# Paged attention in a hybrid decoder step: the transposed, scaled probabilities made by transposes and an add, in place of a matmul with a scaled pattern

## The chip, the core and the metric

The kernel runs on one core of a Trainium2 chip, in one launch. The metric is the device time of a whole execution in microseconds (us), the median of several runs. A core has a matmul engine (TensorE, PE in the profile, with its weight loads as PEld), a vector engine (VectorE, DVE), a scalar engine (ScalarE, ACT), GpSimd (POOL), a sync engine that issues DMAs (SyncE, SP) and 16 DMA engines. Each engine takes its instructions in program order and waits on semaphores where another engine's result is needed. PE writes only to PSUM, eight banks of 512 fp32 columns on 128 partitions.

## The reference

Two layers of a decoder step over 256 prompt rows and 64 sample rows (8 sequences of 8 tokens), width 2048. A layer projects its input with one matrix, runs three mixers side by side, projects their outputs, and ends with a gated feed-forward block. The change is in the second mixer, for the sample rows:

```
# _diff_attn_sample, 4 heads, two maps of 64 dims per head, 1024 cached keys in 8 pages
s_past = einsum('bqhmd,bkhmd->bhmqk', q, k_past) * scale
s_new  = einsum('bqhmd,bkhmd->bhmqk', q, k) * scale
p  = softmax(concat([s_past, s_new]))            # with a causal mask on the new keys
pd = p[:, :, 0] - lam * p[:, :, 1]               # the two maps
o  = einsum('bhqk,bkhv->bqhv', pd[..., :P], v_past) + einsum(..., pd[..., P:], v)
```

The other two mixers are a gated delta rule (six heads) and a gated linear attention (six heads, "GLA"). The output projection starts with the outputs of the delta rule and of this attention, and needs those of GLA for its second half.

## The kernel before

**Dense work.** All weight matrices stream through SBUF in blocks of 128x512 fp32, 217 of them for a layer's input projection and 1618 in all; one of each layer's 217 is in a form of its own and not split. A block is split into a high and a low part, `whi` by a cast on ScalarE and `wlo` by a subtraction on VectorE (line 1021), and used by 12 matmuls of 320 columns, high by high, high by low and low by high. These are the *dense* matmuls here, PE rows with `whi` or `wlo`. Blocks are loaded some eight ahead of use and split three or four ahead.

**Mixers.** The mixers are generators that advance between the dense matmuls while the program is written. They never stand still for each other in the text; what orders them is data, SBUF space and PSUM banks. The cached-key attention (`attn_scores`, line 2049, and `attn_values`, line 2121) takes the eight sequences in four pairs. For a pair it computes scores on 128 partitions (head, sequence, map, query), exponentiates into `e` (128x1088: 1024 cached keys and 64 new ones), and then needs `PT`: keys on the partitions, 64 columns (sequence, head, query), scaled by the softmax sums and with the two maps subtracted. Before the change one matmul for each page does that at once: `e` is the stationary operand and the moving one is a 128x64 pattern of zeros and ones whose rows are scaled. `attn_values` multiplies `PT` with the cached values, two pairs at a time ("a quad"), page by page as the value pages land in a ring of three buffers.

**What follows the attention.** The delta rule of the sample rows, `gdn_sample` (line 1795), is run for two groups of three heads. In the second group the score products `sq,sk` of its third head are written to the PSUM bank that the attention's last transpose has left, and GLA (`gla_main`, line 2172) takes the SBUF space that the attention frees. After its scores and a small triangular inverse, `gdn_sample` takes its three heads in turn in one buffer of 128x1024: the head's state is loaded, multiplied (`gen,sq` and `gen,sk`), updated, stored, and the next one is loaded over it. GLA takes levels (1, 2, 4 and so on), each with subtractions, an exponential, multiplications, some 60 small products and predicated copies. A last step, `gate` (line 1533), multiplies the delta rule's output with its gate into `oA`.

**Order.** When all instructions are recorded, `Program.order` (line 536) sorts them with a list scheduler that uses the costs and latencies written in the file, and `issue` (line 691) emits them in that order on every engine. A dense matmul therefore has a fixed place among the mixers' matmuls, and PE does not go past one that waits. The first dense matmul of the output projection reads `oA`; it stands behind the 216 dense blocks of the input projection, that is behind 2592 dense matmuls.

```
            for f in ((("oA", l), ("oB", l)) if hf == 0 else (("oC", l),)):
                drain(f)
```

Of the kernel before, what the change touches and what calls it, by code (L numbers as in the profile page):

```python
# [18 lines left out]
ALU = mybir.AluOpType  # L19
# [49 lines left out]
def shape_consts(past_len):  # L69
    c = Cols()  # L70
    p = np.arange(128)
    j, i = p[:, None], p[None, :]
    c.add("ident", np.eye(128))
    c.add("tri", j <= i)
    c.add("tri16", (j <= i) / 16.0)
    j8, i8 = np.arange(64)[:, None], np.arange(128)[None, :] % 64
    same8 = (j8 // 8) == (i8 // 8)
    c.add("tri8d", same8 & (j8 <= i8))
    c.add("bo8d", same8)
    c.add("tri8_16", (same8 & (j8 <= i8))[:, :64] / 16.0)  # L80
    c.add("ind8", ((p[:, None] % 64) // 8) == np.arange(8)[None, :])
    c.add("mneg", np.where(i >= j, 0.0, NEG))
    c.add("mneg8", np.where((same8 & (i8 >= j8))[:, :64], 0.0, NEG))
    mcz = np.zeros((128, 256))
    mcz[:, 128:] = np.where(i <= j, 0.0, NEG)
    c.add("mcz", mcz)
    j32, i32 = p[:, None] % 32, np.arange(32)[None, :]
    ms = [(j32 // (2 * s) == i32 // (2 * s)) & (j32 % (2 * s) < s) & (i32 % (2 * s) >= s) for s in (1, 2, 4, 8, 16)]
    c.add("ms", np.stack(ms, 1))
    c.add("m4", ((p[:, None] % 32) // 8) == np.arange(4)[None, :])  # L90
    h, b2, m, q = p // 32, (p // 16) % 2, (p // 8) % 2, p % 8
    cc = np.arange(64)
    c.add("pat", (b2[:, None] == cc[None] // 32) & (h[:, None] == (cc[None] // 8) % 4) & (q[:, None] == cc[None] % 8))
    c.add("sel0", m[:, None] == 0)
    c.add("sel1", m[:, None] == 1)
    t = np.arange(64)
    mnew = [np.where((t[None] // 8 == 2 * pr + b2[:, None]) & (t[None] % 8 <= q[:, None]), 0.0, NEG) for pr in range(4)]
    c.add("mnew", np.stack(mnew, 1))
    c.add("idb", j32 == i32)
    inv = (1.0 / (np.float32(500000.0) ** (np.arange(8, dtype=np.float32) * np.float32(2.0) / np.float32(16.0)))).astype(np.float32)  # L100
    pos = np.concatenate([np.arange(NPR), np.tile(past_len + np.arange(8), 8)]).astype(np.float32)
    ang = (pos[:, None] * inv[None, :]).astype(np.float32)
    cos, sin = np.cos(ang).T, np.sin(ang).T
    C, S = np.ones((128, NT)), np.zeros((128, NT))
    for mm in range(2):
        C[64 * mm:64 * mm + 8] = cos
        C[64 * mm + 8:64 * mm + 16] = cos
        S[64 * mm:64 * mm + 8] = -sin
        S[64 * mm + 8:64 * mm + 16] = sin
    c.add("cos", C)  # L110
    c.add("sin", S)
    c.add("e6", np.full((128, 1), 1e-6))
    c.add("e5", np.full((128, 1), 1e-5))
    c.add("one", np.ones((128, 1)))
    c.add("mhalf", np.full((128, 1), -0.5))
    c.add("i2048", np.full((128, 1), 1.0 / 2048))
    c.add("i512", np.full((128, 1), 1.0 / 512))
    ci = Cols()
    ci.add("mi", np.stack([j32 == i32] + ms, 1))
    return c, ci  # L120
# [623 lines left out]
def emit(nc, pool, psp, T, O, coff, ioff, n_pages):  # L744
# [7 lines left out]
    NPG = n_pages // 8  # L752
# [22 lines left out]
    banks = [psp.tile([128, 512], F32, name=f"bank{i}") for i in range(8)]  # L775
# [32 lines left out]
    def cs(name, rows=slice(0, 128)):  # L808
        a, n = coff[name]
        return cst[rows, a:a + n]  # L810


    def mm(out, lhsT, rhs, start=True, stop=True):
        PE.matmul(out, lhsT, rhs, start=start, stop=stop, skip_group_check=True)

    def tr(out, in_, rows=slice(0, 128)):
        k = rows.stop - rows.start
        a, _ = coff["ident"]
        PE.transpose(out, in_, cst[rows, a + rows.start:a + rows.start + k])

    def tt(eng, out, a, b, op):
        eng.tensor_tensor(out=out, in0=a, in1=b, op=op)
# [4 lines left out]
    def tsc(eng, out, a, s1_, op0, s2_=None, op1=None):  # L827
        if s2_ is None:
            eng.tensor_scalar(out=out, in0=a, scalar1=s1_, scalar2=None, op0=op0)
        else:  # L830
            eng.tensor_scalar(out=out, in0=a, scalar1=s1_, scalar2=s2_, op0=op0, op1=op1)
# [73 lines left out]
    def bank(n=1):  # L905
        if clk.task.t > clk.t["PE"] + SLACK:
            yield
        while len(dense_free if wide[0] else mix_free) < n:
            yield WAIT
        bs = [(dense_free if wide[0] else mix_free).popleft() for _ in range(n)]  # L910
        for b_ in bs:
            prog.epoch(f"bank{b_}")
        return bs if n > 1 else bs[0]

    def fb(*bs):
        for b in bs:
            free_dense(b)
# [1131 lines left out]
    def attn_scores(l, lsel, getb, get1):  # L2049
        X = L  # L2050
        q, ring = X["kv"]
        EH = yield from get1(1024 + 64 + 64)
        e = ap(EH)
        QDs = []
        for i in range(2):
            QD = yield from getb(256)
            G.memset(ap(QD), 0.0)
            QDs.append(QD)
        X["PT"] = {}
        X["PTfree"] = deque()  # L2060
        for i in range(2):
            X["PTfree"].append((yield from getb(576)))
        for pr in range(4):

            qd = ap(QDs[pr % 2]).rearrange("p (h e c) -> p h e c", h=4, e=2)
            for e2 in range(2):
                for m in range(2):
                    r = slice(64 * m, 64 * m + 64)
                    c = e2 * 16 + m * 8
                    t0 = 256 + (2 * pr + e2) * 8  # L2070
                    (G if m else V).tensor_copy(qd[r, :, e2, c:c + 8], blkB[r, 0:4, t0:t0 + 8])
            yield
            bs = yield from bank(2)
            for pg in range(0, NPG, 2):
                for b2 in range(2):
                    KT = yield from kv_next(q[0])
                    kt = ap(KT).rearrange("p (a h t) -> p h a t", a=2, h=4)
                    c0 = (pg % 4) * 128
                    for h in range(4):
                        mm(banks[bs[pg // 4]][32 * h:32 * h + 32, c0:c0 + 256], qd[:, h, b2, :], kt[:, h], b2 == 0, b2 == 1)  # L2080
                    ring.append(KT)
                yield
            bn = yield from bank()
            for b2 in range(2):
                for h in range(4):
                    mm(banks[bn][32 * h:32 * h + 32, 0:64], qd[:, h, b2, :], blkB[:, 4 + h, 256:320], b2 == 0, b2 == 1)
            sm = yield from getb(8)
            s = ap(sm)
            for i in range(2):
                V.tensor_reduce(out=s[:, i:i + 1], in_=banks[bs[i]], op=ALU.max, axis=AX.X)  # L2090
            tt(V, e[:, 1024:1088], banks[bn][:, 0:64], cs("mnew")[:, pr * 64:pr * 64 + 64], ALU.add)
            fb(bn)
            V.tensor_reduce(out=s[:, 2:3], in_=e[:, 1024:1088], op=ALU.max, axis=AX.X)
            V.tensor_reduce(out=s[:, 3:4], in_=s[:, 0:3], op=ALU.max, axis=AX.X)
            tsc(V, s[:, 3:4], s[:, 3:4], -0.125, ALU.mult)
            for i in range(2):
                A.activation(e[:, 512 * i:512 * i + 512], banks[bs[i]], AF.Exp, scale=0.125, bias=s[:, 3:4], accum_out=s[:, i:i + 1])
            A.activation(e[:, 1024:1088], e[:, 1024:1088], AF.Exp, scale=0.125, bias=s[:, 3:4], accum_out=s[:, 2:3])
            fb(*bs)
            V.tensor_reduce(out=s[:, 4:5], in_=s[:, 0:3], op=ALU.add, axis=AX.X)  # L2100
            V.reciprocal(s[:, 5:6], s[:, 4:5])
            tt(V, s[:, 5:6], s[:, 5:6], lsel, ALU.mult)
            tsc(V, e[:, 1088:1152], cs("pat"), s[:, 5:6], ALU.mult)
            fr(sm)
            yield
            while not X["PTfree"]:
                yield WAIT
            PT = X["PTfree"].popleft()
            pt_ = ap(PT)
            bb = yield from bank(2)  # L2110
            for pg in range(NPG):
                mm(banks[bb[0]][:, pg * 64:pg * 64 + 64], e[:, pg * 128:pg * 128 + 128], e[:, 1088:1152])
            mm(banks[bb[1]][0:64, 0:64], e[:, 1024:1088], e[:, 1088:1152])
            A.copy(pt_[:, 0:512], banks[bb[0]])
            V.tensor_copy(pt_[0:64, 512:576], banks[bb[1]][0:64, 0:64])
            fb(*bb)
            X["PT"][pr] = (PT, clk.task.t)
            yield
        set_flag(("asc", l))
# [514 lines left out]
```

## Time and profile before

| | |
|---|---|
| median of 3 runs | 3294.72 us (3292.67 to 3296.1) |
| the profiled execution, its own time | 3294.52 us |
| its span, first to last instruction | 3292.7 us |
| PE busy | 3235.2 us (98%) |
| VectorE, ScalarE, GpSimd busy | 1959.6, 1493.2, 359.7 us |
| mean granted clock of TensorE | 0.994 |

The span is what the trace covers; 1.8 us of the execution's time lie around it. A busy PE is the union of its instructions' times, and their ends overlap, so the distance between two starts tells more of PE's pace than the time of one.

### The profile page before, as it was taken

Reading aid. Unit: us, or ns where it says so; the run is one execution under the profiler, and the core shown is the slowest. Engines: PE = TensorE matmul, PEld = TensorE weight load, DVE = VectorE, ACT = ScalarE, POOL = GpSimd, SP = SyncE. Lnnn points to the kernel's source line nnn. Section 1 sums busy time; section 2 is a strip of 40 time slices with the busy share of each in tenths; the row PEclk is TensorE's granted clock in tenths of the full one; section 3 lists DMA queues with packets and bytes.
Section 4 is the critical chain, followed back from the end, with each engine's and each line's share of the span. In section 5 each row is a group of like instructions: output and inputs, shape, how many; then the busy total and the mean of one; then the engine's idle time right before and its main releaser. Section 6 shows DMA issues by size and latency. Waiting matters only on the chain.

```text
span 3292.7 us, 67703 instructions
## 1 busy us (share of the span) xinstructions
PE 3235.2 (98%) x25466; PEld 3072.3 (93%) x25466; DVE 1959.6 (60%) x3780; ACT 1493.2 (45%) x3069; POOL 359.7 (11%) x604
## 2 busy tenths in 40 slices
PE   9999999999999999999999999989999999999997
PEld 9987887899999999999999887878999999999997
DVE  5676558885444445544776764588854544454446
ACT  5454444465433443344574444444744334433444
POOL 0233323200000000000002333231000000000000
PEclk9999999999999999999999999999999999999998
DMA  7466764455555555555555667534555555555553
GB/s 228 142 194 212 220 194 129 137 148 157 151 149 150 151 151 148 151 150 151 150 154 154 193 217 231 170 127 138 147 151 151 151 149 150 151 150 149 150 151 115
DMA packets 264393, 527.70 MB, mean 160 GB/s; under 512 B 31362, under 2 KB 33026, under 8 KB 263938
## 3 DMA queue, kind: packets, MB, share of 16 engines
q1 hardware_dynamic: 243586, 456.26, 48.4%
q0 software_dynamic: 20480, 67.13, 6.3%
q8 instruction: 199, 3.26, 0.4%
q14 instruction: 128, 1.05, 0.1%
HBM read 506.25 MB, written 16.36 MB: 159 GB/s over the span
## 4 chain that ended last, share of the span: by engine, by line
PE 76%; issue 2%; DVE 1%; DMA 1%; ACT 0%; POOL 0%; POOLq 0%; SPq 0%; ACTq 0%; DVEq 0%
PE bank L696 76%; DVE gen L696 0%; POOLq L2029 0%; DMA geng<-in_ck 0%; DVE wlo L696 0%; DVE geng L696 0%; POOL geng L2031 0%; DVE blkB L696 0%; DMA out_gs<-gen 0%; DMA gen<-in_sgdn 0%; DMA c<-in_sgdn 0%; ACT blkB L696 0%; DVE c L696 0%; POOL blkB L696 0%; ACT accq L696 0%
## 5 line engine op out<-in xcount | busy, mean ns | idle before, releaser
L696 DVE TENSOR_TENSOR wlo<-raw,whi 128x512 fp32r<-128x512 f32 x1616 | 1124.2, 696 | 1091.4 <-PE bank L696 893.5
L696 ACT CAST whi<-raw 128x512 fp32r<-128x512 f32 x1616 | 1001.7, 620 | 1403.6 <-PE bank L696 1340.0
L696 PE MATMUL bank<-xh,wlo 128*128 128x320 f32 (+1 forms) x4544 | 1418.6, 312 | 0.0
L696 PE MATMUL bank<-xh,whi 128*128 128x320 f32 (+1 forms) x4544 | 1413.3, 311 | 4.7 <-ACT xh L696 4.7
L696 PE MATMUL bank<-xl,whi 128*128 128x320 f32 (+1 forms) x4544 | 1414.6, 311 | 0.1
L696 PEld LDWEIGHTS bank<-xh,whi 128*128 128x128 f32 x4544 | 856.1, 188 | 12.8 <-issue 5.7
L696 PEld LDWEIGHTS bank<-xh,wlo 128*128 128x128 f32 x4544 | 857.8, 189 | 7.6 <-issue 3.9
L696 PEld LDWEIGHTS bank<-xl,whi 128*128 128x128 f32 x4544 | 855.4, 188 | 7.6 <-issue 4.4
L696 PE MATMUL bank<-actA,whi 128*128 128x320 f32 x1152 | 255.5, 309 | 0.0
L696 PEld LDWEIGHTS bank<-actA,whi 128*128 128x128 f32 x1152 | 192.9, 188 | 0.4
L696 PE MATMUL bank<-actA,wlo 128*128 128x320 f32 x576 | 178.1, 309 | 0.0
L696 PE MATMUL bank<-actB,whi 128*128 128x320 f32 x768 | 170.5, 309 | 0.0
L696 PE MATMUL bank<-actCh,whi 128*128 128x320 f32 x448 | 138.3, 309 | 0.0
L696 PE MATMUL bank<-actCl,whi 128*128 128x320 f32 x448 | 138.3, 309 | 0.0
L696 PE MATMUL bank<-actCh,wlo 128*128 128x320 f32 x448 | 138.3, 309 | 0.0
L696 PEld LDWEIGHTS bank<-actB,whi 128*128 128x128 f32 x768 | 128.6, 188 | 0.0
L696 PE MATMUL bank<-actB,wlo 128*128 128x320 f32 x384 | 118.6, 309 | 0.0
L696 PE MATMUL bank<-geng,gen 128*32 128x256 f32 (+5 forms) x968 | 101.8, 466 | 7.3 <-DMA geng<-in_ck 4.4
L696 PEld LDWEIGHTS bank<-actA,wlo 128*128 128x128 f32 x576 | 108.2, 188 | 0.1
L696 POOL COPY gen<-g 128x24 f32<-128x24 f32 x18 | 5.9, 328 | 878.1 <-DMA g<-in_scv 871.2
L2031 POOL DMA_DIRECT2D geng<-in_ck x128 | 70.7, 552 | 274.3 <-DVE actA L696 137.8
L696 PE MATMUL bank<-oA,whi 128*128 128x320 f32 x384 | 92.7, 325 | 5.3 <-ACT oA L696 4.8
(291 smaller groups left out, 3324.1 us busy)
## 6 DMA issues: line engine op xcount, KB each, us to landing
raw<-in_wgu SPq DMA_DIRECT2D x704, 256.0 KB
raw<-in_win SPq DMA_DIRECT2D x434, 256.0 KB
raw<-in_wd SPq DMA_DIRECT2D x352, 256.0 KB
geng<-in_ck POOLq DMA_DIRECT2D x128, 256.0 KB, 3.8
geng<-in_cvp POOLq DMA_DIRECT2D x128, 256.0 KB, 3.7
raw<-in_wout SPq DMA_DIRECT2D x128, 256.0 KB
c<-in_sgdn SPq DMA_DIRECT2D x6, 512.0 KB
out_gs<-c SPq DMA_DIRECT2D x6, 512.0 KB
```

Source lines behind the costliest of these rows:

```text
L696: fn(*[real(x) for x in a], **{k: real(v) for k, v in kw.items()})
L2031: G.eng.dma_start(out[:, k * 512:k * 512 + 512], src[l, ds(reg, 1)].rearrange(pat))
```

## The change

The scaled pattern goes. VectorE scales all of `e` by the per-row factor (128x1088, in place), PE transposes it with the identity, four pages to a bank, and the two maps are joined when they leave the bank: ScalarE copies the columns of map 0 and VectorE adds those of map 1, once for each of the two sequences. The new keys (64 columns) take a third bank. So for each of the four pairs of each layer: 9 pattern matmuls become 9 transposes; one ScalarE copy of 512 columns and one VectorE copy of 64x64 become six copies and six additions; one VectorE scaling of 64 columns becomes one of 1088.

```diff
-            tsc(V, e[:, 1088:1152], cs("pat"), s[:, 5:6], ALU.mult)
+            tsc(V, e[:, 0:1088], e[:, 0:1088], s[:, 5:6], ALU.mult)
...
-            bb = yield from bank(2)
-            for pg in range(NPG):
-                mm(banks[bb[0]][:, pg * 64:pg * 64 + 64], e[:, pg * 128:pg * 128 + 128], e[:, 1088:1152])
-            mm(banks[bb[1]][0:64, 0:64], e[:, 1024:1088], e[:, 1088:1152])
-            A.copy(pt_[:, 0:512], banks[bb[0]])
-            V.tensor_copy(pt_[0:64, 512:576], banks[bb[1]][0:64, 0:64])
-            fb(*bb)
+            for c0, n, k in [(512 * i, 128, 4) for i in range(NPG // 4)] + [(1024, 64, 1)]:
+                bb = yield from bank()
+                b = banks[bb][0:n, 0:128 * k]
+                for i in range(k):
+                    tr(b[:, 128 * i:128 * i + 128], e[:, c0 + n * i:c0 + n * i + n])
+                mv = b.rearrange("p (a h b m q) -> p b m a h q", a=k, h=4, b=2, m=2)
+                pv_ = pt_[0:n, c0 // 2:c0 // 2 + 64 * k].rearrange("p (a b h q) -> p b a h q", a=k, b=2, h=4)
+                for b2 in range(2):
+                    A.copy(pv_[:, b2], mv[:, b2, 0])
+                    tt(V, pv_[:, b2], mv[:, b2, 1], pv_[:, b2], ALU.add)
+                fb(bb)
```

`e` shrinks by 64 columns and the constant `pat` (64 columns) is gone. No other line changes, but the recorded program is sorted anew, and its order changes from the first pair of a layer to the output projection.

**SP, the end of layer 0's input projection.** `raw` is a weight block (217 of `in_win`, then `in_wout`), `gen<-in_wa` a GLA weight, `gen<-in_sgdn` the state of a head for `gdn_sample`. Both pieces begin where 193 and 211 blocks have been issued. Before:

```order
L696 DMA gen<-in_wa 128x384
L696 DMA raw<-in_win 128x512 x9
L696 DMA gen<-in_sgdn 128x1024
L696 DMA raw<-in_win 128x512 x5
L696 DMA out_gs<-gen 128x1024
L696 DMA raw<-in_win 128x512
L696 DMA gen<-in_sgdn 128x1024
L696 DMA raw<-in_win 128x512 x7
L696 DMA out_gs<-gen 128x1024
L696 DMA raw<-in_win 128x512
L696 DMA gen<-in_sgdn 128x1024
```

And now:

```order
L694 DMA raw<-in_win 128x512 x4
L694 DMA gen<-in_wa 128x384
L694 DMA raw<-in_win 128x512 x2
L694 DMA raw<-in_wout 128x512 x5
L694 DMA gen<-in_sgdn 128x1024
L694 DMA raw<-in_wout 128x512 x4
L694 DMA out_gs<-gen 128x1024
L694 DMA gen<-in_sgdn 128x1024
L694 DMA out_gs<-gen 128x1024
L694 DMA gen<-in_sgdn 128x1024
L694 DMA out_gs<-gen 128x1024
```

The first state of the second group is loaded behind 222 blocks where it was behind 202, and from the first store to the third load no weight block is issued any more, where 9 were.

**PE, the second head's state products in layer 0.** `gen,sq` and `gen,sk` are the products of the loaded state, `geng 32x32` the small products of GLA's levels, `xh`, `xl` with `whi`, `wlo` dense matmuls. Before, 2403 dense matmuls of the layer stand ahead of the first of these products:

```order
L696 MATMUL bank_81<-xl,whi 128x320
L696 MATMUL bank_81<-xh,wlo 128x320
L696 MATMUL bank_86<-gen,sq_625 32x512
L696 MATMUL bank_86<-gen,sk_91 32x512
L696 MATMUL bank_86<-gen,sq_625 32x512
L696 MATMUL bank_86<-gen,sk_91 32x512
L696 MATMUL bank_84<-cst,sk_91 64x128
L696 MATMUL bank_84<-cst,sv 64x128
L696 MATMUL bank_81<-xh,whi 128x320
L696 MATMUL bank_81<-xl,whi 128x320
```

Now all 2592 do, and up to the first product with `oA` only mixers' rows follow; this is the end of that stretch, from the third head's update on:

```order
L694 MATMUL bank_84<-gen 64x128
L694 MATMUL bank_86<-gen 128x512
L694 MATMUL bank_85<-gen 128x512
L694 MATMUL bank_82<-geng 32x32 x6
L694 MATMUL bank_83<-geng 32x32 x6
L694 MATMUL bank_84<-geng 32x32 x6
L694 MATMUL bank_82<-cst,gen 128x64 x3
L694 MATMUL bank_83<-geng 32x32 x6
L694 MATMUL bank_79<-oA_6178,whi 128x320 x2
```

In dense matmuls that stand ahead, layer 0: the third head's scores (`sq,sk 64x64`) 2237 before and 2485 now; the first head's state products 2333 and 2569; the second's 2403 and 2592; the third's 2509 and 2592; the first product with `oA` 2592 in both. Layer 1 repeats all of these counts (9696 matmuls later, for all but `sq,sk`, which differ in the same 248).

**VectorE, the last value product of layer 0's attention.** `wlo<-raw,whi` is the split of a weight block, `gen<-bank,cst 128x512` the mask on the finished value products of the second quad. Before:

```order
L696 SCALAR_TENSOR_TENSOR gen<-gen,bank_85 128x128 x3
L696 TENSOR_TENSOR g_0_90<-g_0_90,gen 128x3 x2
L696 TENSOR_SCALAR g_0_90<-g_0_90 128x3
L696 TENSOR_TENSOR gen<-bank_82,cst 128x512
L696 TENSOR_TENSOR wlo<-raw,whi 128x512
L696 TENSOR_REDUCE gen<-gen 128x128
```

And now:

```order
L694 TENSOR_TENSOR g_0_90<-g_0_90,gen 128x3
L694 TENSOR_TENSOR g_0_90<-g_0_90 128x384
L694 TENSOR_TENSOR wlo<-raw,whi 128x512 x2
L694 SCALAR_TENSOR_TENSOR gen<-bank_83,gen 64x128
L694 TENSOR_TENSOR wlo<-raw,whi 128x512 x13
L694 TENSOR_TENSOR gen<-bank_82,cst 128x512
```

The mask stands behind 205 blocks where it stood behind 184, and 13 blocks in a row have no mixer's instruction on VectorE among them.

## Rows read from the trace of the kernel before

**Rows 1.** The page: PE's busy time; busy tenths and clock in 40 slices.

```profile
PE 3235.2 (98%) x25466; PEld 3072.3 (93%) x25466; DVE 1959.6 (60%) x3780; ACT 1493.2 (45%) x3069; POOL 359.7 (11%) x604
...
PE   9999999999999999999999999989999999999997
...
PEclk9999999999999999999999999999999999999998
```

**Rows 2.** Busy us by stage: stretch, length, PE, PEld, DVE, ACT, POOL, clock, DMA share.

```profile
400.00:465.00 65.00, 65.00 (x655) 53.58 (x655) 30.18 (x74) 24.54 (x58) 21.37 (x39) 1.00 0.68 220
497.60:562.60 65.00, 57.78 (x923) 48.18 (x923) 51.74 (x102) 30.45 (x64) 24.75 (x22) 1.00 0.42 130
578.00:586.00 8.00, 6.33 (x42) 5.08 (x41) 5.32 (x10) 2.54 (x14) 0.62 (x1) 0.79 0.11 40
2128.00:2193.20 65.20, 59.10 (x925) 49.37 (x923) 51.85 (x102) 30.54 (x64) 24.43 (x18) 0.97 0.41 130
```

**Rows 3.** Timeline of PE: two dense starts, 22 dense matmuls apart.

```profile
541.23 0.31 PE L696 MATMUL bank<-xh,whi 128*128 128x320 f32 x1
...
544.47 0.31 PE L696 MATMUL bank<-xl,whi 128*128 128x320 f32 x1
```

**Rows 4.** Timeline of PE, layer 0's end: start, duration, idle before.

```profile
497.60 0.59 PE L696 MATMUL bank<-gen,sq 128*32 128x512 f32 x1
...
514.99 0.62 PE L696 MATMUL bank<-gen,sq 128*32 128x512 f32 x1
...
538.64 0.59 PE L696 MATMUL bank<-gen,sq 128*32 128x512 f32 x1 [1.51 <-DMA gen<-in_sgdn]
...
555.73 0.24 PE L696 MATMUL bank<-cst,gen 64*128 64x64 f32 x1 [1.24 <-DVE gen L696]
...
562.63 0.41 PE L696 MATMUL bank<-oA,whi 128*128 128x320 f32 x1 [2.48 <-ACT oA L696]
```

**Rows 5.** The same two ends in layer 1.

```profile
2128.15 0.62 PE L696 MATMUL bank<-gen,sq 128*32 128x512 f32 x1
...
2193.25 0.41 PE L696 MATMUL bank<-oA,whi 128*128 128x320 f32 x1 [2.31 <-ACT oA L696]
```

**Rows 6.** Timeline of VectorE, SP and PE: links of one state, and the last addition.

```profile
498.72 0.69 DVE L696 TENSOR_TENSOR gen<-bank,cst 128x512 f32<-128x512 f32 x1 [1.11 <-PE bank L696]
...
507.07 1.28 DVE L696 TENSOR_TENSOR gen<-gen,bank 128x512 f32<-128x512 f32 x2
...
508.42 0.34 SPq L696 DMA_DIRECT2D out_gs<-gen  x1
...
511.28 0.38 SPq L696 DMA_DIRECT2D gen<-in_sgdn  x1
...
551.34 0.69 DVE L696 TENSOR_TENSOR gen<-gen,bank 128x512 f32<-128x512 f32 x1
```

**Rows 7.** Groups of VectorE in 497.6 to 562.6: count, busy us, mean ns.

```profile
L696 DVE TENSOR_TENSOR wlo<-raw,whi 128x512 fp32r<-128x512 f32 x21 | 14.7, 701 | 5.9 <-PE bank L696 4.1 <-issue 0.8 <-ACT gen L696 0.7
```

**Rows 8.** PE: pattern matmuls (two records each), value products, six transposes, dense starts behind.

```profile
405.16 1.90 PE L696 MATMUL bank<-geng 128*128 128x64 f32 x16
406.87 0.39 PE L696 MATMUL bank<-xl,whi 128*128 128x320 f32 x1
...
416.83 0.64 PE L696 MATMUL bank<-geng,gen 128*32 128x512 f32 x4
...
423.56 0.64 PE L696 MATMUL bank<-geng,gen 128*32 128x512 f32 x4
...
478.65 0.83 PE L696 MATMUL bank<-cst,gen 128*128 128x128 f32 x6
479.24 0.39 PE L696 MATMUL bank<-xh,wlo 128*128 128x320 f32 x1
```

**Rows 9.** Groups of VectorE and ScalarE that read a bank: count, busy us, mean ns.

```profile
L696 DVE TENSOR_TENSOR gen<-bank,cst 128x256 f32<-128x256 f32 x16 | 6.8, 425 | 11.6 <-PE bank L696 11.5
L696 ACT COPY gen<-bank 128x256 f32<-128x256 f32 x26 | 9.6, 368 | 3.7 <-PE bank L696 2.9 <-DVE wlo L696 0.7
```

More of the change, by code (lines that the diff above doesn't have):

```diff
@@ L91, in shape_consts @@
     h, b2, m, q = p // 32, (p // 16) % 2, (p // 8) % 2, p % 8
-    cc = np.arange(64)
-    c.add("pat", (b2[:, None] == cc[None] // 32) & (h[:, None] == (cc[None] // 8) % 4) & (q[:, None] == cc[None] % 8))
     c.add("sel0", m[:, None] == 0)
@@ L2051, in attn_scores @@
         q, ring = X["kv"]
-        EH = yield from get1(1024 + 64 + 64)
+        EH = yield from get1(1024 + 64)
         e = ap(EH)
```

## The prediction

> **What bounds the kernel now.** I read the page first: PE is busy for 98% of the span and granted full clock nearly throughout [rows 1]. The reader should see that no stage can be shortened except by taking work or waiting from PE. Next come the stages: from 400 to 465 us PE is busy for all of 65.0 us, but from 497.6 to 562.6 only for 57.78, and in the same stage of layer 1 for 59.10 of 65.20 [rows 2]. So PE waits only in a few short places, and the last stretch before the output projection is one. The timeline says on what: the second group of `gdn_sample` takes its first state at 497.60, its second at 514.99 and its third at 538.64, the last after 1.51 us of waiting for the load; its final transposes wait 1.24 us for VectorE, and the first dense matmul with `oA` starts at 562.63 after 2.48 us of waiting for ScalarE [rows 4]. This chain and the dense work of the input projection end together. Dense matmuls lie in its gaps, so its 65.03 us cost little. Layer 1 has the same two ends, 2128.15 and 2193.25, 65.10 us apart [rows 5].
>
> **The change, part by part.** *PE's own work.* Eight pattern matmuls push the next dense one back: from 405.16 to 406.87, 1.71 us [rows 8]; with the one for the new keys, two records more at 1.71/16 = 0.11 us, 1.92 us for a pair. Six transposes take from 478.65 to 479.24, 0.59 us [rows 8], 0.10 us each; nine are 0.89 us, and I add 0.2 us for each of two further handovers between mixers and dense work (an estimate: the first dense matmul behind a group takes 0.39 us and one in the stream 0.31 [rows 3, 8], doubled for the way in). So about 0.6 us less for a pair, 2.5 us for a layer; I count 1 to 2.5, and use 1, since two of the three groups are smaller and their fills less well shared.
>
> *VectorE and ScalarE.* The additions read 256 elements a partition from a bank, 425 ns as the nearest row has it, the copies 368 ns [rows 9]. A pair gets four such additions (1.7 us), two small ones and a wide scaling, some 3 us on VectorE, and four such copies for one of 512 on ScalarE, about 1 us more. From 400 to 465 VectorE is busy for 30.18 us of 65 and ScalarE for 24.54 [rows 2]: as busy time this is hidden. As latency it is not: it makes `PT` later, and `PT` is what the value products wait for. Without that cover the additions alone would cost 4 x 1.7 = 7 us a layer.
>
> *The order.* This is the term that counts. The attention's last value product moves back by about 21 weight blocks, as VectorE's order shows, and takes the second group of `gdn_sample` and GLA with it: 2569 dense matmuls stand ahead of the first state product where 2333 stood, 236 more. A dense matmul takes (544.47 - 541.23)/22 = 0.147 us [rows 3], so these are 34.8 us. The mixers' work ahead of that product is otherwise the same set, less the 1 us above. The first state product therefore starts at 497.6 + 34.8 - 1 = 531.4 us, if PE is never left waiting until then.
>
> Behind it only 2592 - 2569 = 23 dense matmuls (3.4 us) are left to lie in the chain's gaps, where 259 (38.2 us) lay. So the dense matmul with `oA` starts one chain length X after 531.4. X is not in the trace of before and is bounded from both sides. Above by what it was, 65.0 us [rows 4]: the same steps in the same order with more PE work between. Below by its links without any dense matmul between: for one state the products start at 497.60 and the two additions end at 507.07 + 1.28 = 508.35 [rows 6], 10.75 us, of which some 2.5 us are spent behind dense matmuls; store and load take from 508.42 to the next product at 514.99, 6.57 us [rows 4, 6]; from the last addition's end, 551.34 + 0.69 = 552.03, to `oA` are 10.60 us [rows 4, 6]. With 8.2 us for a state: 3 x 8.2 + 2 x 6.57 + 10.6 = 48.3 us. VectorE gives another floor: it is busy for 51.74 us in this stage [rows 2], of which 14.7 us are 21 splits of weight blocks [rows 7]; the other 37 us all remain, so that the links will queue on VectorE behind GLA's. I take X = 55, nearer to 48 than to 65 since the dense work goes almost entirely, and above it for that queue.
>
> So `oA` is used at 531.4 + 55 = 586.4 us, 23.8 us later than at 562.6, and PE is idle for as much. *Clock.* Where PE waits much the granted clock falls: 578 to 586, with PE busy for 6.33 of 8 us, shows 0.79 in the mean, so part of it lies at 1.2 GHz and (1 - 0.79) x 8 = 1.7 us are lost [rows 2]. After a stage with far more waiting I allow 2 us a layer (0 to 5). One layer: 25.8 us; layer 1 has the same counts and the same 65.1 us [rows 5], so 51.6 us for both.
>
> **The sum** is made against the profiled execution, 3294.5 us (0.2 us from the median of the runs, so the same for both): 3294.5 + 51.6 = **3346 us**. By the bounds: X = 48.3, the PE saving at 2.5 us (a start at 529.9) and no loss of clock give 3294.5 + 2 x (529.9 + 48.3 - 562.6) = 3326 us; X = 65 and 5 us of clock give 3294.5 + 2 x 38.8 = 3372 us.
>
> That nothing dense can slip past the waiting matmuls shows in the waits of 1.24 and 2.48 us, with dense work behind them in the order [rows 4]. The Trainium skill, "TensorE: Matmul & The Clock Gate", section "Part 2: What happens when you issue a matmul", says that matmuls stay in program order and only weight loads are pulled ahead. By that rule the trace agrees; if it did not hold, the idle time above would be filled and the first rival would be right.
>
> **The rivals.** *The tail is hidden, and the change pays by its transposes.* The chain runs so much faster without dense work between that it ends as early as before. Break-even is X = 562.6 - 531.4 = 31.2 us; at X = 28 the time would be 3294.5 - 2 x 3.2 = 3288 us, faster; about 31 gives 3294. Against it: VectorE alone has 37 us of other work there [rows 2, 7], and two round trips and the end, 13.1 + 10.6 us, hold no dense work to be saved [rows 4, 6].
>
> *PE waits before the tail as well.* Value products come as their pages land, 6.73 us apart at present (416.83 and 423.56 [rows 8]). Now there are four or five blocks between two of them, 55 x 0.147 + 1.07 (a group of eight) = 9.2 us, so loads would have to be over a third slower to hold PE. The transposes wait for a scaling and two reads of the bank; 3 us of waiting at each of eight pairs would add 24 us: 3370 us, and more with 6 us: 3394.
>
> *Transposes bring the clock down.* The six at 478.65 stand in a stretch between dense matmuls, like the new ones, and the stage before shows a granted clock of 1.00 [rows 2, 8]. If each of the 24 groups did cost one dip of 1.7 us, the time would be 3346 + 41 = 3387 us. The Trainium skill, "TensorE: Matmul & The Clock Gate", section "Part 4: PE-mode transpose", says that a transpose does not count as PE being busy in the way of a matmul, which speaks for this; no row here shows such a dip at a group between dense matmuls.
>
> **How the numbers follow.** The forecast, 3326 to 3372, gets 0.76: the order is fixed and the links are measured. PE waiting before the tail gets 0.10, the clock 0.03, a milder tail (X from 36 to 48, 3304 to 3326) 0.03. No change (X about 31) gets 0.05 and faster 0.03. The range 3320 to 3380 holds the first and part of the second and fourth, some 0.8; its own reach for the likeliest case is 3326 to 3372. About 0.2% (6.6 us) is what a measurement of this kernel can tell from no change: faster 0.03, the same 0.05, slower 0.92.
>
> **What would show it.** Right: two stretches, ahead of the first product with `oA` in each layer, in which PE is busy for less than half of some 50 us, with waits put down to VectorE and to the load of the state; first state products about 34 us later than before, spaced by 14 to 18 us; a lower granted clock there and just after; the dense stages unchanged. Wrong: state products within 10 us of their former times; or PE idle spread over the attention, with waits on scaled `e` or value pages; or dips of the clock at the transposes.

## The result and the profile after

The changed kernel takes 3350.15 us (median of 4 runs, 3344.49 to 3351.97), the kernel before, beside it on the same chip, 3295.41 (4 runs, 3292.67 to 3296.62): a ratio of 1.0168, 95% interval 1.0153 to 1.0183, slower by 54.7 us. The profiled execution took 3351.97 us; its span of 3350.3 us is 57.6 longer than before.

The page: busy times, and busy tenths and clock in 40 slices, to be held against [rows 1].

```profile
PE 3244.7 (97%) x25394; PEld 3072.6 (92%) x25394; DVE 1977.6 (59%) x3820; ACT 1500.4 (45%) x3109; POOL 356.4 (11%) x604
...
PE   9999997899999999999999999969999999999997
...
PEclk9999997999999999999999999979999999999998
```

PE is busy for 9.5 us more than before, so by far most of the 57.6 us is waiting. It lies in two neighbouring slices of layer 0 (7 and 8 tenths) and in one of layer 1 (6). The stages of layer 0 (stretch, length, PE, PEld, DVE, ACT, POOL, clock, DMA share, GB/s), first in large pieces and then around the fall of the clock:

```profile
200.00:400.00 200.00, 195.80 (x1853) 160.21 (x1852) 132.91 (x358) 95.55 (x288) 69.18 (x134) 1.00 0.64 202
...
534.56:586.52 51.96, 29.01 (x696) 16.16 (x696) 35.58 (x78) 16.87 (x39) 22.52 (x18) 0.60 0.23 73
586.52:1761.26 1174.74, 1166.14 (x7958) 1152.62 (x7958) 688.33 (x1171) 538.78 (x1004) 29.30 (x47) 0.99 0.52 148
...
660.00:1640.00 980.00, 980.00 (x6682) 979.52 (x6682) 530.27 (x886) 425.56 (x743) 1.17 (x2) 1.00 0.54 151
...
540.00:545.00 5.00, 3.07 (x38) 1.41 (x37) 3.79 (x7) 2.60 (x6) 2.02 (x2) 1.00 0.21 52
...
546.00:590.00 44.00, 22.24 (x528) 11.68 (x529) 30.52 (x67) 15.07 (x35) 18.79 (x18) 0.50 0.18 66
590.00:593.00 3.00, 3.00 (x13) 3.00 (x12) 2.96 (x10) 1.95 (x4) 0.66 (x1) 0.50 0.00 0
```

The reader should see that the long dense stage behind (660 to 1640) has no hole, and that 23.0 of the 52 us of the chain, from the first state product to the first `oA`, are idle, at a mean clock of 0.60; before, 7.2 of 65.0 were, at 1.00 [rows 2]. The timeline of PE names the steps, to be held against [rows 4, 5]:

```profile
415.62 1.08 PE L694 MATMUL bank<-geng,gen 128*32 128x256 f32 x8 [2.43 <-DMA geng<-in_ck]
...
534.56 0.59 PE L694 MATMUL bank<-gen,sq 128*32 128x512 f32 x1 [0.34 <-DMA gen<-in_sgdn]
...
546.60 1.85 PE L694 MATMUL bank<-geng 64*32 64x32 f32 x120 [3.28 <-DVE geng L694]
...
552.24 1.06 PE L694 MATMUL bank<-gen,sq 128*32 128x512 f32 x1 [2.88 <-DMA gen<-in_sgdn]
...
568.25 1.03 PE L694 MATMUL bank<-gen,sq 128*32 128x512 f32 x1 [1.69 <-DMA gen<-in_sgdn]
...
586.52 0.64 PE L694 MATMUL bank<-oA,whi 128*128 128x320 f32 x1 [3.57 <-ACT oA L694]
588.90 0.63 PE L694 MATMUL bank<-oA,whi 128*128 128x320 f32 x1 [1.74 <-DVE oA L694]
...
591.99 0.73 PE L694 MATMUL bank<-oA,whi 128*128 128x320 f32 x2
...
592.79 0.58 PE L694 MATMUL bank<-oA,whi 128*128 128x320 f32 x2
...
593.36 0.46 PE L694 MATMUL bank<-oB,whi 128*128 128x320 f32 x2
...
593.80 0.46 PE L694 MATMUL bank<-oB,whi 128*128 128x320 f32 x2
...
2194.63 0.59 PE L694 MATMUL bank<-gen,sq 128*32 128x512 f32 x1 [0.88 <-DMA gen<-in_sgdn]
...
2246.49 0.64 PE L694 MATMUL bank<-oA,whi 128*128 128x320 f32 x1 [3.56 <-ACT oA L694]
```

The links of layer 0's chain on VectorE (the additions that end each state) and on SP (the two stores that a load waits for), to be held against [rows 6]:

```profile
544.46 1.28 DVE L694 TENSOR_TENSOR gen<-gen,bank 128x512 f32<-128x512 f32 x2
...
560.50 1.28 DVE L694 TENSOR_TENSOR gen<-gen,bank 128x512 f32<-128x512 f32 x2 [1.78 <-PE bank L694]
...
580.52 0.69 DVE L694 TENSOR_TENSOR gen<-gen,bank 128x512 f32<-128x512 f32 x1
...
545.82 0.34 SPq L694 DMA_DIRECT2D out_gs<-gen  x1
...
561.84 0.34 SPq L694 DMA_DIRECT2D out_gs<-gen  x1
```

The first state product stands at 534.56 (497.60 before), the first dense matmul with `oA` at 586.52 (562.63 before): 23.9 us later. What layer 0 costs in all is read at the next layer's first `sq,sk`, behind the same work in both kernels:

The kernel before, with its window from the first `oA` to there:

```profile
1731.27 0.33 PE L696 MATMUL bank<-sq,sk 128*64 128x64 f32 x2
...
562.63:1731.27 1168.64, 1164.09 (x7954) 1150.37 (x7954) 683.46 (x1166) 537.91 (x1004) 30.84 (x43) 1.00 0.53 149
```

The kernel after:

```profile
1761.26 0.33 PE L694 MATMUL bank<-sq,sk 128*64 128x64 f32 x2
```

Layer 0 costs 30.0 us, layer 1 the other 27.6; in layer 1 the first `oA` comes 53.2 us later than in [rows 5], 23.2 of them its own. What PE waited for in the whole span (us in total, times, longest):

```profile
PE bank L694 <- DVE geng L694: 18.6, 13, 3.3
PE bank L694 <- DVE gen L694: 17.3, 12, 2.4
PE bank L694 <- DMA gen<-in_sgdn: 10.6, 6, 3.2
```

The waits for the states (`in_sgdn`) and on VectorE are the predicted ones. What PE waited for from 240 us, ahead of the first pair's scaling in layer 0, to 534:

```profile
PE bank L694 <- DMA geng<-in_ck: 4.6, 3, 2.4
PE bank L694 <- DVE g L694: 0.9, 1, 0.9
PE bank L694 <- DMA gen<-in_wa: 0.3, 1, 0.3
```

Scaled `e` (a `geng` written by VectorE) and `PT` (a `gen`) aren't among them.

### The profile page after: what moved, and what is told of

Same layout as the page of the kernel before. It is cut to its first block, busy times and chain, and to the rows that moved or that the text cites. A ratio compares the mean times of both kernels' runs of the same rounds, so it can differ in the third digit from the quotient of the medians.

```text
span 3350.3 us, 67689 instructions
## 1 busy us (share of the span) xinstructions
PE 3244.7 (97%) x25394; PEld 3072.6 (92%) x25394; DVE 1977.6 (59%) x3820; ACT 1500.4 (45%) x3109; POOL 356.4 (11%) x604
## 3 DMA queue, kind: packets, MB, share of 16 engines
q14 instruction: 130, 1.06, 0.1%
## 5 line engine op out<-in xcount | busy, mean ns | idle before, releaser
L694 PE MATMUL bank<-oA,whi 128*128 128x320 f32 x384 | 95.3, 331 | 10.6 <-ACT oA L694 7.1
```

The costliest lines, as they stand in the source:

```text
L694: fn(*[real(x) for x in a], **{k: real(v) for k, v in kw.items()})
```

## The experiments

My theory (A): the change costs what it does because the end of the attention, and with it the second `gdn_sample` group, stands later in PE's order, so that its chain outlasts the dense work of the input projection. Rivals: (B) the added work of VectorE and ScalarE, or PE waiting for it, is the cost; (C) the transposes bring the clock down. The place of the first state product is counted in blocks of 12 dense matmuls that stand ahead of it in PE's order; `oA` is first used behind 216. None of these kernels leaves out part of the computation.

**1. The three banks of a pair at once.** In the changed kernel:

```diff
-            for c0, n, k in [(512 * i, 128, 4) for i in range(NPG // 4)] + [(1024, 64, 1)]:
-                bb = yield from bank()
+            b3 = yield from bank(3)
+            for bb, (c0, n, k) in zip(b3, [(512 * i, 128, 4) for i in range(NPG // 4)] + [(1024, 64, 1)]):
```

> The changed kernel with one thing altered: a pair asks for its three PSUM banks at once and then issues its nine transposes together; every instruction is the same. In the order of the program the third sq,sk of layer 0's second gdn_sample group then stands behind 189.0 blocks of 12 dense matmuls, where it stood behind 186.4 before the change and 207.1 after it; its first state product stands behind 199.5 (194.4 before, 214.1 after; the first oA behind 216 in all). Theory A (the place in the order costs the time): first state product at 497.6 + (199.5 - 194.4) x 12 x 0.147 = 506.6 us, the chain behind it 61 to 63 us (between 52 of the changed kernel and 65 of the one before, by the dense work left in its gaps), so first oA at 567 to 570, and 3295 to 3308 us in all. Rival B (the added work of VectorE and ScalarE, or PE waiting for it at the transposes): the same work is still there, so 3340 to 3355 us. Rival C (transposes bring the clock down): nearly as B, 3335 to 3355 us, with dips of the granted clock where the groups of transposes stand.

Measured: 3315.88 us, ratio 1.0056 (1.0036 to 1.0076). The same instructions, issued from another place, give back 34 of the 55 us. B and C don't allow that; but A expected 8 us less. Its places came out (timeline of PE):

```profile
508.93 0.62 PE L694 MATMUL bank<-gen,sq 128*32 128x512 f32 x1
...
572.54 0.63 PE L694 MATMUL bank<-oA,whi 128*128 128x320 f32 x1 [0.67 <-ACT oA L694]
...
2219.22 0.90 PE L694 MATMUL bank<-cst,blkC 128*128 128x128 f32 x3 [4.79 <-ACT geng L694]
2219.94 0.63 PE L694 MATMUL bank<-oA,whi 128*128 128x320 f32 x1
```

Layer 0 fits to within 2.5 us (506.6 and 567 to 570 expected). In layer 1 the chain takes 72.8 us, from 2147.19 to 2219.94, and matmuls on `blkC` that wait for ScalarE (4.79 us) stand ahead of the dense one with `oA`; the rest of the 9 us over layer 0's 63.6 isn't taken apart. The place of the first state product isn't all; what else stands ahead of `oA` counts too.

**2. The kernel before with its banks split.** Pattern matmuls and all, but three banks, one after the other:

```diff
-            bb = yield from bank(2)
-            for pg in range(NPG):
-                mm(banks[bb[0]][:, pg * 64:pg * 64 + 64], e[:, pg * 128:pg * 128 + 128], e[:, 1088:1152])
...
+            for c0, n, k in [(512 * i, 128, 4) for i in range(NPG // 4)] + [(1024, 64, 1)]:
+                bb = yield from bank()
+                for i in range(k):
+                    mm(banks[bb][0:n, 64 * i:64 * i + 64], e[:, c0 + n * i:c0 + n * i + n], e[:, 1088:1152])
+                (A.copy if k > 1 else V.tensor_copy)(pt_[0:n, c0 // 2:c0 // 2 + 64 * k], banks[bb][0:n, 0:64 * k])
+                fb(bb)
```

> The kernel before (pattern matmuls, e not scaled, no additions) with one thing altered: its pattern products are written to three banks that are asked for one after the other (4, 4 and 1 pages), each evicted by itself, as the transposes of the changed kernel are. In the order, layer 0's first state product stands behind 203.4 blocks of 12 dense matmuls (194.4 before, 214.1 after). Theory A: first state product at 497.6 + 9.0 x 12 x 0.147 = 513.5 us, the chain behind it 58 to 61 us, first oA at 571 to 575, in all 3310 to 3324 us, slower than before though no operation of the change is in it. Rival B (the cost is the added work of VectorE and ScalarE): 3294 to 3299 us, as before. Rival C (the transposes): 3294 to 3299 us.

Measured: 3324.49 us, ratio 1.0086 (1.0069 to 1.0103), half a us above A's range. The kernel has no scaling of `e`, no transpose for a map and no addition, and yet has half of the loss. Timeline of PE:

```profile
514.29 0.59 PE L696 MATMUL bank<-gen,sq 128*32 128x512 f32 x1 [1.14 <-DMA gen<-in_sgdn]
...
571.51 0.64 PE L696 MATMUL bank<-oA,whi 128*128 128x320 f32 x1 [4.83 <-ACT oA L696]
```

513.5 and 571 to 575 were expected. So three requests in turn are a good part of what moves the order: at each (`bank`, line 903 of the changed kernel) a mixer whose planned time lies ahead of PE's gives up its turn.

**3. The scaling alone.** In the kernel before, with the pattern matmuls on the unscaled pattern:

```diff
-            tsc(V, e[:, 1088:1152], cs("pat"), s[:, 5:6], ALU.mult)
+            tsc(V, e[:, 0:1088], e[:, 0:1088], s[:, 5:6], ALU.mult)
```

> The kernel before with the scaling of the change alone: VectorE scales all of e (1088 columns in place of the 64 of the pattern), and the pattern matmuls take the unscaled pattern. In the order, layer 0's first state product stands behind 197.5 blocks of 12 dense matmuls (194.4 before, 214.1 after). Theory A: first state product at 497.6 + 3.1 x 12 x 0.147 = 503 us, first oA at 564 to 567, in all 3297 to 3304 us. Rival B (the added work of VectorE is the cost): the scaling is the largest single one of the added operations, eight to a layer, so a good part of the 55 us that the change cost, 3310 to 3330 us. Rival C (the transposes): as before, 3294 to 3299 us.

(A layer has four pairs and so four scalings, not eight.) Measured: 3318.29 us, ratio 1.0062 (1.0044 to 1.0081): A missed by 14 us, and B's number came. The two layers part, though. Timeline of PE, layer 0's chain:

```profile
506.20 0.59 PE L696 MATMUL bank<-gen,sq 128*32 128x512 f32 x1
...
573.60 0.63 PE L696 MATMUL bank<-oA,whi 128*128 128x320 f32 x1 [4.24 <-ACT oA L696]
```

Windows of the same kernel (columns as above), each layer's chain and the stretch behind it:

```profile
506.00:573.60 67.60, 56.84 (x847) 45.63 (x846) 50.54 (x97) 29.23 (x62) 24.84 (x22) 0.91 0.39 118
573.60:640.00 66.40, 57.76 (x380) 48.41 (x381) 51.85 (x87) 26.01 (x70) 16.41 (x12) 0.88 0.31 95
...
2152.70:2216.50 63.80, 53.80 (x846) 43.97 (x846) 50.40 (x97) 29.17 (x62) 25.11 (x19) 0.95 0.42 125
2216.50:2283.00 66.50, 59.14 (x409) 48.34 (x410) 55.79 (x95) 27.01 (x70) 17.86 (x11) 0.94 0.36 104
```

The chains take 67.4 us and 63.8 with the same order, and the granted clock is 0.91 and 0.88 in layer 0, 0.95 and 0.94 in layer 1. By (1 - clock) x length, which counts PE's waiting too, that is a loss of at most 14 us in the one and 7 in the other. The kernel before, read in the same way, loses 3 and 5: nothing and 2 us in the chains [rows 2], and 3.3 us in the 66 us behind each, at a clock of 0.95. So part of A's miss may be clock; the place alone (197.5) doesn't give the time. Run 6 settles whether the scaling itself costs.

**4. Padded transposes.** Run 1, with the 64 new keys' transpose made a full one (`[(1024, 128, 1)]` for `[(1024, 64, 1)]`, `e` 64 columns wider).

> The changed kernel with its three banks asked for at once, as in the first of these runs, and the transpose of the 64 new keys widened to 128 columns of e (the 64 added ones are zeros and their transposed rows are not read), which takes a different shape out of each pair. The order is nearly that of the first of these runs (first state product behind 200.4 blocks, second 206.4 in place of 205.3). Theory A: 3297 to 3310 us, within 5 us of the first. Rival B: 3340 to 3355 us. Rival C: 3335 to 3355 us.

Measured: 3307.96 us, ratio 1.0036 (1.0023 to 1.0048), in A's range, 8 us below run 1 where 5 were allowed. First state product at 505.99, first `oA` at 570.73.

**5. Nothing changed but two thresholds.** In the changed kernel:

```diff
-        sticky, PB, PW = False, 1000.0, 3000.0
+        sticky, PB, PW = False, 750.0, 2250.0
```

> The changed kernel with not one instruction altered: only the two thresholds by which the scheduler lets small mixer matmuls in among the dense ones (1000 and 3000 ns) are 750 and 2250. In the order, layer 0's first state product then stands behind 190.3 blocks (194.4 before the change, 214.1 after it), the third behind 201.8 (209.1 and 216). Theory A: first state product at 490 to 496 us, first oA at 556 to 564, limited by the dense work or just by the chain, in all 3284 to 3300 us, so all of the 55 us are back. Rival B: 3335 to 3355 us. Rival C: 3335 to 3355 us.

Measured: 3298.67 us, ratio 1.0010 (1.0000 to 1.0020). The loss is gone, all but about 3 us, with every instruction of the change in place. B and C expected 3335 or more. The first state product came at 493.50, as expected, but the first `oA` at 578.62, 15 us later than A allowed. In these 85.1 us PE is busy for 78.44, so that no more is idle than before the change (6.7 us here, 7.2 there): a late `oA` costs as far as PE stands idle, or runs slowly, ahead of it.

**6. The old order with the new operations.** Run 1, and the planner's clock for this mixer set back:

```diff
+            ts_ = clk.task.t
             tsc(V, e[:, 0:1088], e[:, 0:1088], s[:, 5:6], ALU.mult)
+            clk.task.t = ts_
...
             b3 = yield from bank(3)
+            tq = clk.task.t
...
+            clk.task.t = tq
             X["PT"][pr] = (PT, clk.task.t)
```

> Every operation of the change is in it: the three banks are asked for at once, and the planner's clock for this mixer is set back over the scaling and over the group of transposes, copies and additions, so that the mixer's next step is written as early as if these took no time. The computation is the same. In the order, layer 0's first state product stands behind 193.2 blocks of 12 dense matmuls, the next ones behind 199.3 and 208.2 (194.4, 200.2 and 209.1 before the change; 214.1 and 216 twice after it). Theory A (the place in the order costs the time): the order is the old one, so first state product at 494 to 500 us, first oA at 560 to 566, in all 3288 to 3302 us. Rival B (the added work of VectorE and ScalarE, or PE waiting for it): all of it is there, and the order leaves it less room, so 3320 to 3355 us, with waits on the scaled e or on the additions. Rival C (transposes bring the clock down): 3320 to 3350 us with dips at the groups.

Measured: 3290.07 us, ratio 0.9985 (0.9974 to 0.9995): not only is the loss gone, it is below the kernel before, if by no more than 0.05 to 0.26%. Timeline of PE:

```profile
497.40 0.59 PE L694 MATMUL bank<-gen,sq 128*32 128x512 f32 x1 [1.27 <-issue]
...
563.36 0.42 PE L694 MATMUL bank<-oA,whi 128*128 128x320 f32 x1
```

Windows of the same kernel (columns as above), ahead of the chain:

```profile
262.00:270.00 8.00, 6.53 (x58) 5.68 (x58) 4.37 (x14) 1.25 (x3) 5.62 (x9) 0.79 0.85 279
270.00:400.00 130.00, 129.15 (x1362) 104.38 (x1364) 76.50 (x212) 58.11 (x165) 48.41 (x91) 1.00 0.73 229
400.00:497.60 97.60, 94.93 (x1018) 79.28 (x1013) 53.13 (x136) 44.61 (x107) 24.83 (x41) 1.00 0.59 182
```

The state product and `oA` stand where [rows 4] have them. Of the four pairs' transposes of this layer, three lie in the last two windows, at a clock of 1.00; where the clock dips, from 262 to 270, PE has waited 2.28 us for keys. The first pair's (245.6 to 247.0) stand ahead of that dip, with the clock at 1.00 over 240 to 262. This run refutes B and C as causes of the 55 us.

**7. The kernel before with earlier mixers.** The line of run 5 with 500.0 and 1500.0, in the kernel before; **8.** the same line in run 6.

> The kernel before, its instructions unaltered, with the same two thresholds at 500 and 1500 ns. First state product behind 172.2 blocks, third behind 185.5, so that 30 blocks (54 us) of dense work are left for the end of the chain. Theory A: first state product at about 458 us, the chain ends some 20 us ahead of the dense work, no wait for oA and no low clock at the end of the input projection; the 7 us of waiting and 3.4 us of clock of each layer are gained in part, 3272 to 3290 us. Rivals B and C say nothing of this run beyond no large change, 3285 to 3300 us; finer mixing could also cost handovers, up to 3310 us.

> The first kernel of this call (all operations of the change, order kept early) with the thresholds of the third (500 and 1500 ns): first state product behind 174.6 blocks (172.2 in the third), so the operations of the change stand against those of before at nearly the same places, away from the end of the chain. Theory A: 0 to 5 us below the third kernel for PE's smaller work (I counted 1 us for a layer, at most 2.5), 3268 to 3290 us. Rival B: 30 to 50 us above the third, with PE waits on VectorE in the attention. Rival C: 20 to 40 us above the third, with dips of the granted clock.

Measured: 3309.74 us, ratio 1.0048 (1.0031 to 1.0064), and 3316.80, ratio 1.0070 (1.0053 to 1.0087). Both missed. `oA` isn't waited for any longer, as expected, but PE is busy for 3242.6 us in the first, 7.4 more than before; I didn't find in which matmuls. The second is 7 us above the first where A had 0 to 5 below, with PE's waits for keys longer, and for states (4.7 us, then 7.7). The first kernel:

```profile
PE bank L696 <- DMA geng<-in_ck: 6.2, 10, 1.4
```

The second:

```profile
PE bank L694 <- DMA geng<-in_ck: 12.2, 13, 3.1
```

Their first state products stand at 465.41 and 475.15, so these operations aren't compared at quite the same places. Earlier is not always better: both are slower than the kernels with 1000 and 3000 ns from which they come, though `oA` no longer waits. The longer waits for loads are part of the second one's loss; the rest of both stays open.

**9. A second buffer for the states.** In the changed kernel, and **10.** the same in run 6:

```diff
-        R2, M2 = yield from private(1920, lambda: (mem if hs else X["memC"][0],))
+        R2, M2 = yield from private(1920 + 1024 * hs, lambda: (mem if hs else X["memC"][0],))
...
+        S0s = [S0, (None, (0, 0, ap(R2)[:, 1920:2944])) if hs else S0]
         for k in range(3):
             h = h0 + k
+            S0 = S0s[k % 2]
```

> The changed kernel with a second buffer of 128x1024 for the states of the second gdn_sample group, so that the load of one state need not wait for the store of the last; the computation is the same. The buffer takes SBUF space from GLA, whose small products move behind the input projection in the order. First state product behind 210.9 blocks of 12 dense matmuls (214.1 without the buffer), so at 534.6 - 3.2 x 12 x 0.147 = 529 us. Theory A (the end of the chain sets the time, and its length is made of its links): the two round trips of store and load, 6.57 us each in the trace of before, and part of the queue behind GLA on VectorE go, so 35 to 41 us from first state product to first oA in place of 52, first oA at 564 to 570 (562.6 before the change, 586.5 after), 10 to 20 us gained for a layer, in all 3305 to 3325 us, if GLA isn't late for the second half of the output projection. Rival B (the chain's length is the queue of added and GLA work on the engines, the round trip is hidden in it): 47 to 52 us, in all 3335 to 3350 us.

> The kernel that keeps the order early (three banks at once, the planner's clock set back) with the second state buffer. First state product behind 194.0 blocks, as without it. Theory A: the chain ends by 545 us, ahead of the dense work, so no wait for oA and no low clock at that place; the few us of waiting that were left there are gained, and GLA's products come later, in the output projection, with waits of their own: 3280 to 3295 us. If GLA becomes late for the second half of the output projection: 3300 to 3320 us.

Measured: 3367.82 us, ratio 1.0212 (1.0195 to 1.0229), and 3327.63, ratio 1.0093 (1.0076 to 1.0110): the times missed, the chain's length came as expected. Timeline of PE in the first:

```profile
520.71 0.62 PE L694 MATMUL bank<-gen,sq 128*32 128x512 f32 x1
...
559.50 0.63 PE L694 MATMUL bank<-oA,whi 128*128 128x320 f32 x1
```

What PE waited for in the whole span of the same kernel:

```profile
PE bank L694 <- DVE gen L694: 31.5, 18, 4.6
...
PE bank L694 <- ACT oCh L694: 5.1, 2, 2.6
```

From the first state product to the return of dense work are 38.8 us in place of 52 (35 to 41 expected); the places came 8 and 5 to 10 us earlier than expected, and nine dense matmuls with `oA` already stand at 532.28. But GLA has lost its space and moved behind; PE now waits for its VectorE steps (`geng`, 16.5 us in the whole span) and for `oCh`, the second half's operand. In run 10 the chain ends early as expected, with `oA` used at 541.03 without a wait and at a clock of 1.00; its loss comes behind, where PE is busy for only 69.21 of the 80 us from 620 to 700. The case that I named as an exception, GLA late, is the one that happened; its time in run 10 is 8 us above the 3300 to 3320 that I gave for it.

**11. The attention recorded first.** Run 6 with the two attention mixers at priority 0 in place of 2 (`spawn(attn_scores(...), 0)`, `spawn(attn_values(...), 0)`).

> The kernel that keeps the order early, with the two attention mixers put first in the recording order of priorities (0 in place of 2). First state product behind 192.2 blocks (193.2 without), third behind 206.1 (208.2). Theory A: as that kernel within 5 us, 3284 to 3296 us. Rival B: no opinion beyond no large change.

Measured: 3307.34 us, ratio 1.0032 (1.0020 to 1.0045): missed by 11 us. PE's waits on VectorE for `geng` are 11.8 us where run 6 has 4.0. Which step of GLA or the inverse comes late there stays open.

Place and time, of all kernels but runs 7 and 8 (chain far earlier) and 9 (nine `oA` matmuls ahead of the chain's end):

```
kernel            blocks ahead of the      first state   first   ratio
                  first state product      product, us   oA, us
run 5             190.3                    493.50        578.62  1.0010
run 11            192.2                    481.79        562.48  1.0032
run 6             193.2                    497.40        563.36  0.9985
run 10            194.0                    488.83        541.03  1.0093
before            194.4                    497.60        562.63  1
run 3             197.5                    506.20        573.60  1.0062
run 1             199.5                    508.93        572.54  1.0056
run 4             200.4                    505.99        570.73  1.0036
run 2             203.4                    514.29        571.51  1.0086
after             214.1                    534.56        586.52  1.0168
```

The place decides between 1.00 and 1.017; among neighbours a difference of some 10 us isn't explained by it, and runs 10 and 11 show that an early place alone isn't enough.

## Why the prediction was right

**The order, 34.8 - 1 us.** The first state product was to come at 531.4 and came at 534.56, 36.96 us later than before. Up to it PE's busy time rose from 488.99 to 521.63 us, by 32.6 where the sum had 33.8, and its idle time by 4.3, for which the sum had nothing; 2.43 of these are one wait for keys (415.62). That the order is the cause is shown by runs 5 and 6: the same operations at the old places cost nothing. What I did not see is why the order moved; run 2 shows that the three bank requests are a good part of it, and runs 1 and 6 that the planned time of copies and additions is another (199.5 blocks, then 193.2).

**The chain, X = 55.** It measured 586.52 - 534.56 = 51.96, and 51.86 in layer 1: inside the bounds of 48.3 and 65, nearer the lower one than I chose. A late start and a short chain cancel, so that `oA` at 586.52, predicted 586.4, is luck. So is part of the length. By the links, the three states took 11.2, 9.5 and 13.0 us where I had put 8.2 each, and the end, from the last addition at 581.21 to `oA`, 5.3 us where I had put 10.6; the two round trips took 6.42 and 6.41, near the 6.57 put down for each. Nine us too little and five too much left the sum near its place, and 48.3 was no floor link by link.

X also held no clock. The products of the first state take 0.59 us each, those of the second and third 1.06, at half the granted clock. In the chain PE is busy for 29.01 us, 3.4 of them for 23 dense matmuls; before, for 57.78 with 38.2 for 259 of them [rows 2]: 25.6 us of mixers' work where it was 19.6. So about 6 us of PE's time are the low clock's (an estimate: it takes the mixers' work for the same), and some of them lie on the chain. One sign that I named didn't come, at least in part for this reason: PE is busy for 56% of the chain, not for less than half. And PE isn't idle for all of the 23.9 us by which `oA` is late: up to `oA` its idle time rose by 20.0 us and its busy time, with no more work, by 3.9.

Run 9 shows that the length isn't fixed: with the round trips of store and load out of the way and GLA behind it, the chain is 13 us shorter. It changes both at once and doesn't say what each is worth.

**The clock, 2 us a layer, allowed 0 to 5.** Behind `oA` comes more than this term: layer 0 costs 30.0 where `oA` is 23.9 late, so 6.1 more, and layer 1 27.6 - 23.2 = 4.4. In layer 0, from the first `oA` to the next layer's first `sq,sk`, PE's busy time rose from 1164.09 to 1166.14, by 2.05 us, and its idle time from 4.55 to 8.60, by 4.05. The 2.05 are the size of the term, and its place can be seen: three dense starts take 0.80 us (591.99 to 592.79) until 593, and 0.44 (593.36 to 593.80) afterwards, so about 1.8 of the 4.1 us from 588.90 to 593.0 are lost. The 4.05 us of waiting had no term, and this is the step of the sum that failed: 1.74 us are waited at 588.90 for VectorE's part of `oA`, where before it was 0.2, and 3.6 for GLA's steps on VectorE (`geng`), where before there were none; other waits are some 1 us shorter. The sum was 51.6, against 57.6 in the spans and 54.7 in the medians.

**PE's own work and VectorE's.** An addition takes 285 ns and a copy 269 (both 128x128 from a bank), where I had taken the rows of 256 elements, 425 and 368; the scaling takes 787 ns. It didn't matter, since run 6 shows that they are hidden. The saving of 1 us a layer isn't measured by itself. That PE's busy time ahead of the first state product rose by 2.1 us less than 236 dense matmuls take is an estimate of it, inside the 1 to 2.5 that I counted; run 6's span is 3.4 us under that of before, with another order.

**The rivals.** The tail did not hide the move: break-even was a chain of 31.2 us, and even with two state buffers it took 38.8. PE did not wait for scaled `e` ahead of the tail: its waits from 240 to 534 are 4.6 us for keys, 0.9 for `g` and 0.3 for weights. The transposes did not bring the clock down: those of three pairs lie between 200 and 400 us, at 1.00. The rule of the Trainium skill, "TensorE: Matmul & The Clock Gate", section "Part 4: PE-mode transpose", that a transpose doesn't count as busy in the way of a matmul, has no price here, where transposes stand between dense matmuls.

## What to carry over

In a program whose order is written by a planner, read first what a change does to the order: the operations here cost nothing at the old places and 55 us at the new ones, and two thresholds gave that back. Where a chain and a block of independent work end together, count the independent work that is left behind the chain's start; less than the chain is long is idle time. A shortened chain only helps up to the next one: look who takes the space and the engine that it leaves.

## What the runs showed of the hardware

The granted clock stayed low past the waiting that brought it down. From 540 to 545, with PE busy for 3.07 of 5 us, it was still 1.00; PE then waited for 3.28 us, up to 546.60, and from 546 to 593 it was 0.50, the level of 1.2 GHz. That holds 44 us (546 to 590) in which PE was busy for half of the time, and 3 us (590 to 593) in which it was busy throughout with dense matmuls 0.267 us apart (0.80/3). At 593 it went back to 1.00 and 0.147 us. The low level was paid twice: by the dense matmuls behind the wait, and by the chain's own matmuls, whose state products took 1.06 us where they took 0.59 at 1.00.

In experiment 3 the same order and the same work ran at a clock of 0.91 in one layer and 0.95 in the other. The clock isn't a fixed addition to a stage, and differences of some 7 us between neighbouring orders can't be read as the worth of an operation.
